# Cross attention of a decoder layer by two matrices made once, in place of query, score, gather and output products

## The chip, the cores and the metric

The kernel runs on one core of one Trainium2 chip. The metric is the device time of one execution in microseconds; lower is better. The core's engines are named as in the profile: PE (matrix products) with PEld (its weight loads), DVE (vector engine), ACT (scalar engine), POOL, and SP, which here only issues transfers. A queue name such as SPq or ACTq stands for the instructions by which an engine issues transfers.

## The reference

One layer of a decoder is computed for a prompt of 1024 tokens and for 8 samples of one token each, all in fp32. The layer has three stages with a residual add behind each: a mixer (attention with forget gates beside a gated unit, then an output projection), cross attention into 256 memory tokens with 4 heads of width 256, and a gated feed-forward network (FFN). The change concerns the cross attention of the prompt:

```
mn = rmsnorm(mem, g_mem)
mk = (mn @ w_ck).reshape(B, M, 4, 256)          # also an output
mv = (mn @ w_cv).reshape(B, M, 4, 256)          # also an output
q  = (xn @ w_cq).reshape(B, T, 4, 256)
s  = einsum('bqhd,bmhd->bhqm', q, mk) / 16
p  = softmax(s)
o  = einsum('bhqm,bmhd->bqhd', p, mv).reshape(B, T, 1024)
x  = x + o @ w_co
```

The products can be taken in another order: q·mkᵀ is xn @ (w_cq · mkᵀ), head by head, and o @ w_co is p @ (mv · w_co), head by head. Both inner matrices have 1024 rows and 1024 columns (256 memory tokens for each of 4 heads) and do not depend on the tokens of the prompt.

## The kernel before

The 1024 prompt tokens are worked in two halves of 512, a half being 4 tiles of 128 tokens. The parts follow in this order: p1 (input projections of the whole prompt), the first half's attention with a filler beside it, the second half's attention, then for each half the output projection of the mixer, the cross attention, and the FFN.

**Products.** Most products are done three times in fp32r, with each operand split into a high part and a low part (`gemm3`, lines 272 to 274: high·high, high·low, low·high). `wload` (lines 252 to 262) brings 256 rows by 512 columns of a weight (512 KB, issued by SP at line 249) into a tile `wr` and splits it: ACT makes the high part `wh` (line 235), DVE the low part `wl` (line 236). `split` with a scale uses lines 238 and 239. Products of the cross attention that take no split are plain fp32.

**The memory projection** `pmem` (line 674) makes mk and mv, 512 columns at a time: 4 weight tiles, then 2 products of 8 k-tiles each, evacuated by ACT (line 711) and stored to the outputs `o_mk` and `o_mv` from ACT's queue (line 712). It is the first part of the filler; `gating(0)` (line 618) is the second. The function `mix` runs the filler beside the first half's attention: for each unit of time that the attention's steps announce, `MIXR` units of the filler are traced, with MIXR 1.0. A part announces its units with `yield`; they are planned figures, not microseconds.

**The cross attention** `cross` (line 1120) of one half does, in order: load mk and mv of two heads (`fetch`, lines 1126 and 1128); load w_cq; normalize and transpose the tokens in two parts of 2 tiles each (`norm_T`, line 1090, transposes at line 1106, splits at 238 and 239), where the first of 8 query blocks is multiplied in two halves of 256 columns as soon as each part is there; the other 7 query blocks with 512 tokens moving and the weight stationary, evacuated by ACT at line 1216; for each head transposes of the keys (`keys`, lines 1153 and 1157), scores in plain fp32 (line 1170) with the softmax (`weigh`: DVE maximum at 1172, exponential on ACT, scaling at 1183), transposes of the softmax weights (`turned`, lines 1190 and 1191), and the gather of values in plain fp32 (`gather`, line 1198), whose result is split for the output projection. `out_proj` (line 1015) multiplies by w_co (lines 1055 to 1057 for the first 512 columns, 1073 to 1075 for the rest), adds the residual, sums squares and makes scaled tiles for the FFN's `norm_T`.

**Beside all of it** runs the work of the 8 samples, first `decode` (attention over 8192 cached tokens: a K step loads 1 MB at line 1407 and is two kinds of DVE operation, lines 1423 and 1427 or 1414 and 1415; a V step loads 1 MB at line 1469 and is 8 products of plain fp32 at line 1475, done in groups of two steps), then `sample_rest` (projections of the 8 rows, with weights loaded by POOL). A driver at the end of `build` takes one step of this work whenever the prompt's parts have announced a given number of units:

```
PACE = {'p1': 7.0, 'att0': 12.0, 'attx': 26.0, 'mid0': 8.0, 'ffn0': 8.5, 'att1': 11.0, 'mid1': 6.8, 'ffn1': 2.5, 'rest': 2.9}
```

`att0` is the first half's attention, `attx` its last two head pairs, `mid0` and `mid1` the output projection and the cross attention of a half, `rest` the samples' remaining work. `beside` and `mix` join other parts.

**Order and buffers.** The code traces the work in the order that these generators give; a planner then simulates it with its own costs and sets the order on each engine, taking work that is ready before work that is not. Buffers are rings of fixed length: 18 tiles `u` of 4 KB a partition, 7 tiles `t2` of 2 KB, 4 `wr`, 5 `wh`, 4 `wl`; result banks of PE are `ba` (4 in this part), `bb` (2), `ms` and `dv`. An instruction that needs a tile waits until the ring's oldest is released.

## Time and profile before

| | |
|---|---|
| median of 3 runs | 1817.83 us (1816.76 to 1819.05) |
| profiled execution | 1820.56 us |
| its span, first to last instruction | 1818.4 us |
| mean granted clock of PE in it | 0.986 |
| moved by DMA | 521.06 MB |

The profile is of one execution. Its page gives the busy time of each engine, the groups of instructions by line, and the chain that ended last; views of the trace give the same for a stretch of time, the instructions in order of time (a row is: start, duration, engine, line, operation, out<-in, count, and in brackets the idle time before it with what ended it), who waited for whom (total, times, longest), and the transfers. In the names out<-in, a matrix product's first operand is the moving one, the second the stationary one. The 8 query evacuations of the second half's cross attention end at about 1262, the first output product after it starts at 1295; in the first half the cross attention lies between 547 and 652.

### The profile page before, as it was taken

What the parts mean: (1) busy time and instruction counts of PE and PEld (TensorE: products, weight loads), DVE (VectorE), ACT (ScalarE), POOL (GpSimd) and SP (SyncE); (2) the same over time, 40 slices, a digit from 0 to 9 for tenths busy, and PEclk for the clock granted to TensorE, in tenths of its full rate; (3) what the DMA queues carried; (4) which work ended last, traced back from release to release, by engine and by line L of the source; (5) the groups of instructions that cost most, each with busy time, mean ns of one, the idle gap of its engine ahead of it and who ended that gap; (6) DMA issues with size and microseconds to landing.
All of it is one profiled execution on the core that took longest, in us unless ns stands there. A gap on an engine that the chain in (4) does not pass through costs nothing.

```text
span 1818.4 us, 25090 instructions
## 1 busy us (share of the span) xinstructions
PE 1745.0 (96%) x9637; PEld 1294.9 (71%) x9637; DVE 1397.5 (77%) x1729; ACT 734.4 (40%) x1378; POOL 510.0 (28%) x461
## 2 busy tenths in 40 slices
PE   8999999888998999999999999989899999999997
PEld 5887776656676767777777776766576778767775
DVE  4689668888788877999989899898875549845344
ACT  6332365455643544433333244235353324332332
POOL 1252334332133432223332333334222111011110
PEclk9999999899999999999999999989999999999999
DMA  8886889777696986679878779988787777568982
GB/s 295 306 297 231 302 297 329 242 266 224 219 398 257 342 310 260 257 285 340 316 279 311 271 306 340 381 300 324 290 309 290 267 268 265 179 266 289 359 314 82
DMA packets 157074, 521.06 MB, mean 287 GB/s; under 512 B 20874, under 2 KB 40842, under 8 KB 124186
## 3 DMA queue, kind: packets, MB, share of 16 engines
q0 software_dynamic: 57168, 341.14, 49.5%
q1 hardware_dynamic: 92874, 165.73, 26.4%
q10 hardware_dynamic: 6912, 12.59, 1.8%
q8 instruction: 76, 1.25, 0.3%
q14 instruction: 44, 0.36, 0.1%
HBM read 495.47 MB, written 23.93 MB: 286 GB/s over the span
## 4 chain that ended last, share of the span: by engine, by line
PE 72%; DMA 10%; issue 7%; DVE 6%; ACT 2%; POOL 2%; SPq 0%; POOLq 0%; DVEq 0%; ACTq 0%
PE ba L272 11%; PE ba L274 11%; PE ba L273 11%; PE bb L272 5%; PE bb L273 5%; PE bb L274 5%; PE dv L1475 5%; DMA kv<-cache_k,io 3%; DMA wr<-w_in 2%; DMA kv<-cache_v,io 1%; PE dv L321 1%; PE dv L1751 1%; PE ba L1056 1%; PE ba L1055 1%; PE ba L1057 1%
## 5 line engine op out<-in xcount | busy, mean ns | idle before, releaser
L235 ACT ACTIVATE wh<-wr 128x1024 fp32r<-128x1024 f32 (+2 forms) x220 | 228.9, 1044 | 489.2 <-PE ba L273 156.0
L236 DVE TENSOR_TENSOR wl<-wr,wh 128x1024 fp32r<-128x1024 f32 (+2 forms) x220 | 262.5, 1200 | 175.6 <-PE ba L274 65.7
L1407 POOL DMA_INDIRECT kv<-cache_k,io x128 | 205.6, 1606 | 551.2 <-DVE s L1427 318.9
L1423 DVE TENSOR_TENSOR kv<-kv,d 128x1024 f32<-128x1024 f32 (+1 forms) x156 | 258.0, 1681 | 35.1 <-DMA kv<-cache_k,io 35.1
L1427 DVE TENSOR_REDUCE s<-kv 128x16 f32<-128x1024 f32 (+1 forms) x156 | 258.2, 1674 | 0.1
L1469 POOL DMA_INDIRECT kv<-cache_v,io x128 | 165.3, 1291 | 282.8 <-PE dv L1475 191.8
L272 PE MATMUL ba<-u,wh 128*128 128x512 f32 (+1 forms) x560 | 220.3, 395 | 1.7 <-ACT u L238 1.7
L273 PE MATMUL ba<-u,wh 128*128 128x512 f32 (+1 forms) x560 | 220.2, 393 | 1.7 <-DVE u L239 1.5
L274 PE MATMUL ba<-u,wl 128*128 128x512 f32 (+1 forms) x560 | 219.5, 393 | 0.0
L272 PE MATMUL ba<-wh,u 128*128 128x512 f32 (+1 forms) x495 | 186.9, 379 | 0.9 <-ACT u L235 0.9
L273 PE MATMUL ba<-wl,u 128*128 128x512 f32 (+1 forms) x495 | 185.4, 375 | 1.2 <-DVE wl L236 1.2
L274 PE MATMUL ba<-wh,u 128*128 128x512 f32 (+1 forms) x495 | 183.8, 376 | 0.0
L272 PEld LDWEIGHTS ba<-u,wh 128*128 128x128 f32 x560 | 106.8, 191 | 30.6 <-issue 5.6
L273 PE MATMUL bb<-u,wh 128*128 128x512 f32 (+1 forms) x304 | 119.4, 393 | 9.2 <-DVE u L239 9.2
L274 PEld LDWEIGHTS ba<-u,wl 128*128 128x128 f32 x560 | 106.9, 191 | 29.1 <-issue 6.1
L273 PEld LDWEIGHTS ba<-u,wh 128*128 128x128 f32 x560 | 106.7, 191 | 27.5 <-issue 2.7
L1475 PE MATMUL dv<-kv,s 128*32 128x512 f32 x1024 | 124.2, 598 | 1.8 <-DMA kv<-cache_v,io 1.8
L272 PE MATMUL bb<-u,wh 128*128 128x512 f32 (+1 forms) x304 | 119.4, 393 | 0.0
L274 PE MATMUL bb<-u,wl 128*128 128x512 f32 (+1 forms) x304 | 118.6, 390 | 0.0
L272 PEld LDWEIGHTS ba<-wh,u 128*128 128x128 f32 x495 | 93.0, 188 | 26.0 <-issue 6.9
L274 PEld LDWEIGHTS ba<-wh,u 128*128 128x128 f32 x495 | 92.8, 188 | 21.5 <-issue 3.7
L273 PEld LDWEIGHTS ba<-wl,u 128*128 128x128 f32 x495 | 93.1, 188 | 19.7 <-DVE wl L236 1.9
(425 smaller groups left out, 3255.9 us busy)
## 6 DMA issues: line engine op xcount, KB each, us to landing
wr<-w_up SPq DMA_DIRECT2D x88, 512.0 KB
kv<-w_up POOLq DMA_DIRECT2D x22, 1024.0 KB, 8.0
wr<-w_down SPq DMA_DIRECT2D x40, 512.0 KB
kv<-w_down POOLq DMA_DIRECT2D x11, 1024.0 KB, 8.5
wr<-w_in SPq DMA_DIRECT2D x16, 512.0 KB
wr<-w_o SPq DMA_DIRECT2D x16, 512.0 KB
wr<-w_cq SPq DMA_DIRECT2D x16, 512.0 KB
wr<-w_co SPq DMA_DIRECT2D x16, 512.0 KB
```

Source lines behind the costliest of these rows:

```text
L235: nc.scalar.activation(h, src, AF.Copy)
L236: nc.vector.tensor_tensor(l, src, h.bitcast(F32), op=ALU.subtract)
L272: mmul(out, sh, mh, start=(i == 0), stop=False)
L273: mmul(out, sh, ml, start=False, stop=False)
L274: mmul(out, sl, mh, start=False, stop=(i == n - 1))
L321: mmul(ps[32 * j : 32 * j + 32, :w], xT[:, k, :] if nk == 8 else xT[:, k * 8 : k * 8 + 32], raw[:, q, j * w : (j + 1) * w], start=(k == 0) ...
L1055: mmul(pss[i], mh[k][:, tb], wh, start=(k == korder[0]), stop=False)
L1407: nc.gpsimd.indirect_dma_start(kv, None, a["cache_k"], off(kidx[:, b, ch : ch + 1]))
L1423: nc.vector.tensor_tensor(kvv[:, i : i + m, :], kvv[:, i : i + m, :], qb.unsqueeze(1).broadcast_to((P, m, 512)), op=ALU.mult)
L1427: nc.vector.tensor_reduce(s[:, ch * 4 + i : ch * 4 + i + m, :].rearrange("p k h -> p (k h)"), kvv[:, i : i + m, :].rearrange("p k (h d) -> ...
L1469: nc.gpsimd.indirect_dma_start(kv, None, a["cache_v"], off(kidx[:, b, ch : ch + 1]))
L1475: mmul(dv[32 * j : 32 * j + 32, :], s[:, ch * 4 : ch * 4 + 4, :].rearrange("p k h -> p (k h)"), kvv[:, j, :], start=(ch == 1), stop=(ch == ...
```

## The change

Two matrices are made once, beside the first half's attention, and kept in device memory: `wk_d` (1024 by 1024: for each head, the head's columns of w_cq times the head's keys transposed) and `wv_d` (1024 by 1024: for each head, the head's values times the head's rows of w_co). The cross attention of each half then multiplies the normalized tokens by `wk_d`, which gives the scores of all heads at once, takes the softmax, transposes the weights and multiplies them by `wv_d` in `out_proj`. The kernel gets the transpose of w_cq as one more input, laid out on the host as others are.

In `pmem` each projected block of 512 columns is read back from the output it was stored to (`fetched`, on SP's queue), transposed on PE and split (`turned`), and multiplied: `into_queries` with 256 columns moving, `into_output` with 512. Results are evacuated by ACT and stored from ACT's queue.

```
-MIXR = 1.0
+MIXR = 1.5
...
+        def project(w, dst, n):
...
+        def fetched(src, n):
+            t = U([P, 2, 512])
+            nc.sync.dma_start(t, src[:, n * 512 : (n + 1) * 512].rearrange("(a p) c -> p a c", p=P))
+            return t
+
+        def turned(t):
+            h2, l2 = U([P, 2, 512], F32R), U([P, 2, 512], F32R)
+            for j in range(2):
+                tr = TR()
+                for dd in range(2):
+                    for mt in range(2):
+                        nc.tensor.transpose(
...
+                split(tr, h2[:, j, :], l2[:, j, :])
+                yield 0.5
+            return h2, l2
+
+        def into_queries(n, h2, l2):
+            for j in range(2):
+                for c in range(2):
+                    w = wload(wpair(a["w_cqT"], n * 2 + j, c * 512, 512), 1024)
+                    for q in range(2):
+                        ps = MM()
+                        for i in range(2):
+                            mb = slice((q * 2 + i) * P, (q * 2 + i + 1) * P)
+                            gemm3(
+                                ps[:, i * 256 : (i + 1) * 256],
+                                [
+                                    (w[0][:, d_, mb], w[1][:, d_, mb], h2[:, j, d_ * 256 : d_ * 256 + 256], l2[:, j, d_ * 256 : d_ * 256 + 256])
+                                    for d_ in range(2)
+                                ],
+                            )
+                        t = T2()
+                        nc.scalar.activation(t, ps, AF.Copy)
+                        r0, c0 = c * 512 + q * 256, (n * 2 + j) * 256
+                        nc.scalar.dma_start(
+                            wk_d[r0 : r0 + 256, c0 : c0 + 256].rearrange("(a p) k -> p a k", p=P), t.rearrange("p (a k) -> p a k", k=256)
+                        )
+                    yield 2.9
+
+        def into_output(n, h2, l2):
+            for j in range(2):
+                for c in range(2):
+                    w = wload(wpair(a["w_co"], n * 2 + j, c * 512, 512), 1024)
+                    for mt in range(2):
+                        ps = MM()
...
+                        t = T2()
+                        nc.scalar.activation(t, ps, AF.Copy)
+                        r0 = (n * 2 + j) * 256 + mt * P
+                        nc.scalar.dma_start(wv_d[r0 : r0 + P, c * 512 : (c + 1) * 512], t)
+                    yield 2.9
+
+        for w, dst, into in ((a["w_ck"], mk_d, into_queries), (a["w_cv"], mv_d, into_output)):
+            raws = []
             for n in range(2):
+                yield from project(w, dst, n)
+                raws.append(fetched(dst, n))
+            for n in range(2):
+                h2, l2 = yield from turned(raws[n])
+                yield from into(n, h2, l2)
```

`project` holds what the loop of `pmem` did before. In `norm_T`, what is done behind each of the two parts may now be a generator. In `cross`, tokens are stationary and the matrix moves, 512 columns (two heads) for each of the 4 token tiles; the softmax of a tile follows its product, and the transposes of an earlier tile's weights stand between the products:

```
     def cross(xt, sq):
+        loaded = lambda n: [wload(wpair(wk_d, kk, n * 512, 512), 1024) for kk in range(4)]
+        ws = loaded(0)
...
+        def scores(i, hs, ls):
+            ps, tb = MM(), slice(i * P, (i + 1) * P)
             gemm3(
+                ps,
+                [(hs[k][:, tb], ls[k][:, tb], ws[k // 2][0][:, k % 2, :], ws[k // 2][1][:, k % 2, :]) for k in range(8)],
             )
+            return ps
+
+        def weigh(n, i, ps):
...
+            pp = T2().rearrange("p (j m) -> p j m", m=256)
...
+        def turned():
...
+            split(tr, oh[n, i // 2][:, :, c], ol[n, i // 2][:, :, c])
+
+        def first(hs, ls, c):
+            i0 = c.start // P
+            r = rows_rstd(sq, i0, i0 + 2)
+            nc.vector.tensor_scalar(rq[:, i0 : i0 + 2], r, 1.0 / 16, None, op0=ALU.mult)
+            for i in (i0, i0 + 1):
+                weigh(0, i, scores(i, hs, ls))
                 yield 5.2
+
+        hs, ls = yield from norm_T(xt, G_CROSS, first)
+        ws = loaded(1)
+        for i in range(4):
+            ps = scores(i, hs, ls)
+            turned()
+            weigh(1, i, ps)
+            yield 5.6
+        turned()
...
+        yield from out_proj(wv_d, of, xt, ys=ys, between={0: turned, 1: turned, 2: turned})
```

The functions `fetch`, `products`, `keys` and `gather` go, and with them the query block in memory, the plain fp32 scores and the plain fp32 gather. `out_proj` takes its stationary tiles through a function `of(k, i)` and can call a function behind a given k (`between`). The samples' own cross attention is not changed, and `o_mk` and `o_mv` are written as before.

More of the change, by code (lines that the diff above doesn't have):

```diff
@@ L1112, in norm_T @@
                 yield 0.6
-            first(hs, ls, c)
-            if t0 == 0:
+            more = first(hs, ls, c)
+            if more:
+                yield from more
+            elif t0 == 0:
                 yield 3
@@ L1134, in cross @@
-        q2, ps0 = [], MM()
-        def products(out, ws, dt_, hs, ls, c):
-            cb = slice(dt_ * P, (dt_ + 1) * P)
+        loaded = lambda n: [wload(wpair(wk_d, kk, n * 512, 512), 1024) for kk in range(4)]
+        ws = loaded(0)
+        rq = sm([P, 4], "rq", 2)
+        oh, ol, weights = {}, {}, []
+        def scores(i, hs, ls):
+            ps, tb = MM(), slice(i * P, (i + 1) * P)
             gemm3(
-                out,
-                [(ws[k // 2][0][:, k % 2, cb], ws[k // 2][1][:, k % 2, cb], hs[k][:, c], ls[k][:, c]) for k in range(8)],
-            )
@@ L1224, in cross @@
-        keys(2)
-        fetch(3)
-        turned(0)
-        yield 1
-        weigh(2)
-        yield 3
-        gather(0)
-        yield 4
-        keys(3)
-        turned(1)
-        yield 1
-        weigh(3)
-        yield 3
-        gather(1)
-        yield 4
-        for h in (2, 3):
-            turned(h)
-            yield 1
-            gather(h)
-            yield 4
+                ps,
+                [(hs[k][:, tb], ls[k][:, tb], ws[k // 2][0][:, k % 2, :], ws[k // 2][1][:, k % 2, :]) for k in range(8)],
+            )
@@ new lines, in turned @@
+        def turned():
+            n, i, pp = weights.pop(0)
+            if i % 2 == 0:
+                oh[n, i // 2], ol[n, i // 2] = U([P, 4, 256], F32R), U([P, 4, 256], F32R)
+            c = slice(i % 2 * P, i % 2 * P + P)
+            tr = TR().rearrange("p (k t) -> p k t", t=P)
+            for k in range(4):
+                nc.tensor.transpose(tr[:, k, :], pp[:, k // 2, k % 2 * P : k % 2 * P + P], ident)
+            split(tr, oh[n, i // 2][:, :, c], ol[n, i // 2][:, :, c])
[5 more added lines that the diff above has]
+                weigh(0, i, scores(i, hs, ls))
+                yield 5.2
```

169 lines of the change are left out of this document (55 added, 114 removed).

## The prediction

> **What bounds the kernel now.** I read the page's busy line first, then the windows by stage, the order of time on TensorE (PE), and the waits.
>
> ```profile
> PE 1745.0 (96%) x9637; PEld 1294.9 (71%) x9637; DVE 1397.5 (77%) x1729; ACT 734.4 (40%) x1378; POOL 510.0 (28%) x461
> ```
> ```profile
> 262.00:365.00 103.00, 92.37 (x522) 69.03 (x525) 84.03 (x155) 57.07 (x134) 41.69 (x55) 0.95 0.78 272
> 488.00:547.00 59.00, 58.38 (x309) 44.39 (x308) 48.84 (x60) 26.09 (x45) 17.78 (x12) 1.00 1.00 383
> 547.00:652.00 105.00, 98.36 (x508) 70.35 (x506) 89.00 (x116) 53.18 (x125) 38.52 (x25) 0.97 0.84 316
> 1183.00:1296.00 113.00, 99.67 (x502) 69.78 (x502) 96.00 (x114) 52.72 (x122) 41.71 (x29) 0.94 0.83 306
> 708.00:1110.00 402.00, 398.57 (x1884) 298.60 (x1883) 372.10 (x357) 147.07 (x237) 117.48 (x83) 0.99 0.79 298
> ```
>
> The columns are length, busy PE, weight load, VectorE (DVE), ScalarE (ACT), POOL, then clock, DMA share and GB/s. The rows are the first attention with the memory projection beside it (262 to 365), the first half's output projection, its cross attention, the second half's cross attention, and the first FFN. PE is occupied nearly everywhere, so the sum of PE work sets the time. DVE is next: 0.93 of the FFN row (372.1/402), 0.85 of both cross rows.
>
> A matmul's duration contains its latency. What one costs in a stream is the distance between starts.
>
> ```profile
> 571.86 0.39 PE L272 MATMUL bb<-u,wh 128*128 128x512 f32 x1
> ...
> 576.28 0.40 PE L274 MATMUL ba<-u,wl 128*128 128x512 f32 x1
> ```
> ```profile
> 76.33 0.28 PE L273 MATMUL bb<-wl,u 128*128 128x260 f32 x1
> ...
> 78.00 0.28 PE L272 MATMUL bb<-wh,u 128*128 128x260 f32 x1
> ```
> ```profile
> 633.03 0.63 PE L1153 MATMUL ba<-cp,t 128*128 128x128 f32 x4 [0.34 <-DMA t<-o_mk]
> 633.49 0.60 PE L1190 MATMUL ba<-cp,u 128*128 128x128 f32 x4
> ...
> 635.45 3.72 PE L1170 MATMUL ba<-t,u 128*128 128x256 f32 x16 [0.68 <-ACT t L1157]
> 639.01 1.02 PE L1198 MATMUL bb<-u,t 128*128 128x512 f32 x2
> 639.87 1.02 PE L1198 MATMUL ba<-u,t 128*128 128x512 f32 x2
> ```
>
> In fp32r, 20 starts from 571.86 to 576.28 give 0.233 us for 512 columns. 15 starts from 76.33 to 78.00 give 0.119 for 260 columns, though each shows 0.28. The transposes take 0.115 (0.46/4). Plain fp32 takes two records for one matmul: line 1170 0.2225 each (3.56/16), line 1198 0.43 each (0.86/2).
>
> **What goes, what comes, on PE.** Query products (192 a half), transposes of the weights (32 a half) and output products (192 a half) keep their columns. Gone are the fp32 scores, 64 matmuls, 128 records × 0.2225 = 28.5 us; the fp32 gather, 32 matmuls, 64 × 0.43 = 27.5; and the key transposes, 32 × 0.115 = 3.7. That is 59.7, half of it in each cross stage. New, once, beside the first attention: 192 products of 256 columns × 0.119 = 22.8; 96 of 512 × 0.233 = 22.4; 32 transposes = 3.7. That is 48.9. Net **−11 us**. Were a 256-column product worth its shown duration, 0.28, it would be 54 instead of 22.8 and the net +20; the starts decide, so I take 0.119.
>
> **Waits that go.**
>
> ```profile
> PE bb L1170 <- DVE u L236: 4.2, 1, 4.2
> PE ba L1170 <- ACT t L1157: 1.9, 2, 1.6
> PE bb L1198 <- ACT u L1191: 0.6, 1, 0.6
> PE ba L1198 <- ACT u L1191: 0.6, 1, 0.6
> ```
> ```profile
> 1278.40 3.64 PE L1170 MATMUL bb<-t,u 128*128 128x256 f32 x8 [4.19 <-DVE u L236]
> ```
> ```profile
> PE bb L273 <- DVE u L239: 9.2, 5, 5.6
> ```
>
> The first four rows are all PE waits of the second half's cross products. They lie in the chains keys-scores and transpose-gather, which cease: −7.3. Behind the 4.19 us gap eight records took 3.47 us up to the next start (1281.87), twice the normal, so the gap cost 1.7 more. **−9** in all; the first half's are shorter and not counted. In the new order a weight tile is turned four tiles after its softmax, with 24 products (5.6 us) a tile between, so a turn should wait for nothing. The last row, of the whole execution, is the split of the normalized tiles. Its waits were covered by 24 half products (2.8 us); now two whole score tiles (11 us) stand between the two halves of that part. I take half: **−5**, bounds 0 and −9.
>
> **What the first attention takes on.**
>
> ```profile
> L235 ACT ACTIVATE wh<-wr 128x1024 fp32r<-128x1024 f32 (+2 forms) x220 | 228.9, 1044 | 489.2 <-PE ba L273 156.0
> L236 DVE TENSOR_TENSOR wl<-wr,wh 128x1024 fp32r<-128x1024 f32 (+2 forms) x220 | 262.5, 1200 | 175.6 <-PE ba L274 65.7
> ```
> ```profile
> L711 ACT ACTIVATE t<-ba,rm x5: 687/687/691, 268.5 to 323.6; 128x512 f32<-128x512 f32 x5
> ```
> ```profile
> L712 ACTq DMA_DIRECT2D o_mk<-t x4: 338/342/345, 269.2 to 293.6; - x4
> ```
> ```profile
> DMA packets 14123, 28.05 MB, mean 272 GB/s; under 512 B 1368, under 2 KB 7000, under 8 KB 12579
> ...
> ks_d<-u POOLq DMA_DIRECT2D x12, 128.0 KB, 3.6
> ```
>
> 16 weight loads are split (ACT 16.7 us, DVE 19.2), 32 results evacuated (ACT 22) and stored from ACT's queue (32 × 0.34 = 11), and 8 key and value blocks split (5 each). ACT rises by 55 to 112 us of some 150, DVE from 84 by 24, and by the decode steps below. All of it hides beside PE as long as these engines keep up; uncovered, a part would cost its own length. The higher ratio lets the filler, 41.6 planned units before and about 92 now, last through the whole attention. The gaps of 103 − 92.4 = 10.6 us come partly from the filler running out. I take **−4**, bounds 0 and −10.6. The reads of the two projected blocks wait on SP for the stores. They could hold back the weight loads behind them for one store's landing, some 4 us by the last row above (of half the size), four times. The planner issues what is ready by its own costs, not in the code's order:
>
> ```profile
> 485.39 7.64 SPq L249 DMA_DIRECT2D wr<-w_o  x5
> 493.08 1.12 SPq L1126 DMA_DIRECT2D t<-o_mk  x1
> ...
> 503.36 4.74 SPq L249 DMA_DIRECT2D wr<-w_o  x2
> ```
>
> The load of the memory keys went out amid the w_o loads, which the code asks for first. So I take 0, bound +16. New loads and stores by ACT in the cross stages: none.
>
> **Decode, which is paced by planned units.** The added filler is about 50 units: at 12 and 26 units a step, some 3 steps (bounds 2 and 4) are done earlier. Each cross stage yields about 27 units less: 3.4 steps fewer at 8 in the first, 4 at 6.8 in the second. This only moves work, until the end:
>
> ```profile
> L1475 PE MATMUL dv<-kv,s x144: 592/592/617, 1369.4 to 1432.0; 128*32 128x512 f32 x144
> ```
> ```profile
> 1792.98 0.73 DVE L1804 SCALAR_TENSOR_TENSOR vsum<-vsum,r1r,d 8x512 f32<-8x512 f32 x1
> ```
> ```profile
> 1806.33 1.19 DVE u L1340
> ```
>
> Four steps more remain behind 1363, about 10 units at 2.5. The sample's last result stands 13 us ahead of the prompt's, so I count 0, bound +5.
>
> **DVE in the cross stages.**
>
> ```profile
> L1427 DVE TENSOR_REDUCE s<-kv 128x16 f32<-128x1024 f32 x22 | 26.3, 1212 | 0.0
> L1423 DVE TENSOR_TENSOR kv<-kv,d 128x1024 f32<-128x1024 f32 x22 | 25.9, 1216 | 5.5 <-DMA kv<-cache_k,io 5.5
> ```
>
> Here a key step of decode is two of each, 4.86 us. DVE falls by 3.4 × 4.86 = 16.5 to 72.5, and in the second half by 19.4 to 76.6, while PE falls to about 69. DVE is then the fuller engine. At the FFN's share of 0.926 the two stages need 78 + 83 = 161 instead of 218, a gain of 57, where PE alone would allow 59.7 + 14 = 74. The neighbours at 0.83 can take some. I charge half the difference, **+9**, bounds 0 and +17.
>
> **Sum**: −11 − 9 − 5 − 4 + 9 = −20. The profiled execution took 1820.56 us (span 1818.4), the median of the runs is 1817.83, 0.15% lower: 1800.6, at the median's level **1798**. A difference of 0.2%, 3.6 us, is about what a measurement of this kernel can tell from no change.
>
> **Rivals.**
> *Result buffers run short, slower.* In the first attention the evacuated results use the ring of 7 t2 tiles, with the exponentials and transposes of the attention. Each result holds one for 0.69 + 0.34 + at least 3.6 = 4.6 us; 32 need 147 buffer-us. Their stretch lasts about 62 us (45 of products, 17 of attention: the 47.7 us left of 92.4 after 192 × 0.233, for 70 units, times 31 units). So 2.4 buffers must be free. The attention can hold six (three exponentials, two transposed, one output). With 1.5 free the stretch takes 98 us: +36, net +16, **1834**. It turns slower below 147/(62 + 20) = 1.8 free. For it: ACT is to be the busiest server there. Against: the planner gives buffers by readiness, and before, line 711 waited only for PE.
> The Trainium skill, "DMA: Bandwidth & Descriptors", section "Anatomy of one DMA", puts a DMA at 2.0 us plus its bytes over 436 GB/s, with the receipt from HBM as most of it. That would be an estimated 2.6 us for a store of 256 KB and a threshold nearer 1.4; the trace's 3.6 us for 128 KB is longer.
> *Transfers bind the first attention.* 16 loads and the same bytes stored are 16.8 MB, the blocks read back 2.1, three steps of K and V 6.3: 28 becomes 53.2 MB. At 383 GB/s that is 139 us, less than PE's 103 + 48.9 + 3 − 4 = 151. At 316, the rate of the cross row, it is 168: +17, **1815**, no change. The stage ran at 272, though only because it asked for no more.
> The Trainium skill, same page, section "Bandwidth", gives some 358 GB/s of HBM per core as the limit. By it the stage needs an estimated 149 us, as much as PE. The 383 GB/s row disagrees.
> *DVE binds the cross stages outright*: the whole +17, **1806**.
> *The waits go entirely*: −11 − 9 − 9 − 10.6, **1778**.
>
> **Chances.** Forecast 0.40 (own range 1787 to 1806), DVE 0.15, all waits gone 0.07: faster 0.62. Transfers 0.10: same. Buffers 0.28: slower. The range runs from the best case to the slower one: 1779 to 1834.
>
> **What would show it.** Right: lines of the scores and gather vanish; the cross stages shrink to about 80 us; the first attention grows to about 150 with PE above 0.93; PE's busy sum falls by about 11. Wrong: the first attention beyond 180 us with ACT waiting for t2 tiles or stores; DVE above 0.95 in the cross stages with PE waiting for splits; sample work behind the prompt's last output.

## The result: slower by 25 us

The changed kernel took 1843.49 us (median of 4 runs, 1840.09 to 1846.3), the kernel before in the same comparison 1818.44 (1816.76 to 1822.79): ratio **1.0137**, 95% interval [1.0111, 1.0164]. The forecast was 1798 with a range up to 1834; the time lies outside the range, and the change is slower where faster was forecast. The profiled execution of the changed kernel took 1840.93 us, span 1839.2.

The busy line of its page answers to the one of before:

```profile
PE 1741.9 (95%) x9685; PEld 1297.8 (71%) x9685; DVE 1423.2 (77%) x1769; ACT 754.8 (41%) x1382; POOL 502.8 (27%) x463
```

PE is 3.1 us less busy and the span 20.8 us longer, so PE's idle time grew by 23.9 us. PE's granted clock fell too, from 0.986 to 0.977 in the mean. As an estimate by these means, PE had 1702 us of full-speed work (1741.9 × 0.977) where before had 1721 (1745.0 × 0.986), 19 us less, and at the old clock it would have been busy some 16 us less than it was. No run separates whether the lower clock costs time of its own or only follows the idle time.

The windows say where the time went. A stage begins at the first product of an output projection or at the first transpose of a normalization. First come three stages of before (both attentions; first FFN, here FFN 0; second FFN to the end, here FFN 1), then the same of after, with an output projection and both cross stages; columns as in the prediction.

```profile
262.00:497.10 235.10, 208.27 (x1332) 148.44 (x1332) 193.32 (x341) 138.59 (x310) 78.28 (x102) 0.96 0.74 250
...
706.60:1135.30 428.70, 422.86 (x2019) 315.63 (x2017) 395.33 (x383) 162.36 (x264) 128.34 (x89) 0.99 0.80 300
...
1350.80:1818.40 467.60, 455.75 (x2979) 339.98 (x2977) 266.89 (x403) 157.57 (x287) 71.74 (x101) 0.99 0.70 256
```
```profile
262.00:577.00 315.00, 269.29 (x1692) 197.43 (x1691) 235.77 (x388) 182.31 (x372) 87.99 (x109) 0.93 0.80 275
577.00:627.90 50.90, 50.89 (x227) 38.57 (x228) 45.15 (x57) 13.11 (x23) 20.42 (x12) 0.96 0.86 324
627.90:687.00 59.10, 57.50 (x296) 43.89 (x294) 45.78 (x74) 35.66 (x86) 9.68 (x9) 1.00 0.61 227
...
744.10:1180.90 436.80, 428.05 (x2053) 317.58 (x2053) 408.15 (x398) 164.15 (x265) 139.13 (x96) 0.99 0.83 305
...
1227.70:1290.60 62.90, 60.61 (x313) 44.30 (x311) 52.99 (x77) 34.24 (x81) 22.42 (x17) 0.97 0.69 256
...
1350.60:1839.20 488.60, 468.96 (x3045) 343.25 (x3045) 301.82 (x432) 163.61 (x292) 92.51 (x118) 0.98 0.76 280
```

The cross stages fell from 104.2 and 112.9 us (at these cuts) to 59.1 and 62.9, which is 95 us and more than was forecast. The attentions grew by 79.9, the first FFN by 8.1, the second by 21.0, the output projections and what follows them by 6.9 together. The sum is +20.8. FFN 1 begins at the same time in both (1350.8 and 1350.6): up to there the other stages take back all that the cross stages win, and what is lost on top is lost in FFN 1.

The table counts the decode's key steps in each stage (a step is one key load; one that lies across a cut counts on both sides), and gives the lengths of the same stages in four kernels of the experiments: without the samples' work, and with half of a key step's VectorE work left out. "op" is an output projection: a and c are the mixer's of the two halves, b and d the cross attention's.

| stage | before, us (key steps) | after, us (key steps) | before, no samples | after, no samples | before, half key | after, half key |
|---|---|---|---|---|---|---|
| attentions | 235.1 (15) | 315.0 (18) | 197.8 | 257.6 | 248.4 | 322.2 |
| op a | 50.5 | 50.9 | 46.1 | 45.3 | 47.8 | 49.3 |
| cross 0 | 104.2 (11) | 59.1 (3) | 92.5 | 52.5 | 100.9 | 59.0 |
| op b | 54.8 | 57.1 | 48.4 | 47.5 | 54.8 | 54.0 |
| FFN 0 | 428.7 (42) | 436.8 (46) | 377.9 | 376.5 | 422.1 | 427.3 |
| op c | 47.3 | 46.8 | 44.6 | 44.6 | 48.9 | 48.8 |
| cross 1 | 112.9 (13) | 62.9 (7) | 86.5 | 50.7 | 98.5 | 60.0 |
| op d | 55.3 | 60.0 | 46.6 | 45.8 | 55.1 | 52.0 |
| FFN 1 to the end | 467.6 (0) | 488.6 (6) | 381.9 | 382.0 | 467.2 | 485.5 |

Two readings of the changed kernel's trace belong beside it. All waits of PE in its first cross stage, and then in its second:

```profile
PE bb L274 <- DVE u L1078: 0.9, 1, 0.9
PE ba L274 <- issue: 0.4, 1, 0.4
PE ba L276 <- DVE u L241: 0.3, 1, 0.3
```
```profile
PE bb L276 <- DVE u L241: 2.3, 1, 2.3
```

The chains keys-scores and transpose-gather are gone with their waits. And VectorE's key steps in those stages: in the second cross stage of before, then in the first and the second of after:

```profile
L1423 DVE TENSOR_TENSOR kv<-kv,d 128x1024 f32<-128x1024 f32 x28 | 33.0, 1219 | 8.6 <-DMA kv<-cache_k,io 8.6
L1427 DVE TENSOR_REDUCE s<-kv 128x16 f32<-128x1024 f32 x27 | 31.8, 1208 | 0.0
```
```profile
L1436 DVE TENSOR_TENSOR kv<-kv,d 128x1024 f32<-128x1024 f32 x6 | 7.0, 1212 | 0.0
L1440 DVE TENSOR_REDUCE s<-kv 128x16 f32<-128x1024 f32 x5 | 5.9, 1208 | 0.0
```
```profile
L1440 DVE TENSOR_REDUCE s<-kv 128x16 f32<-128x1024 f32 x12 | 14.3, 1209 | 0.0
L1436 DVE TENSOR_TENSOR kv<-kv,d 128x1024 f32<-128x1024 f32 x12 | 14.1, 1214 | 0.0
```

The first cross stage of before had 22 of each. Of its 52 us of key work (the prediction's rows) 13 are left there, of the second's 65 us 28. That work, 76 us, had to be done elsewhere: by the loads 24 key steps lay in the two stages, now 10.

### The profile page after: what moved, and what is told of

Same layout as the page of the kernel before. It is cut to its first block, busy times and chain, and to the rows that moved or that the text cites. A ratio compares the mean times of both kernels' runs of the same rounds, so it can differ in the third digit from the quotient of the medians.

```text
span 1839.2 us, 25344 instructions
## 1 busy us (share of the span) xinstructions
PE 1741.9 (95%) x9685; PEld 1297.8 (71%) x9685; DVE 1423.2 (77%) x1769; ACT 754.8 (41%) x1382; POOL 502.8 (27%) x463
## 4 chain that ended last, share of the span: by engine, by line
PE 58%; DVE 9%; DMA 4%; issue 4%; ACT 1%; POOL 1%; DVEq 0%; POOLq 0%; ACTq 0%; SPq 0%
PE ba L274 9%; PE ba L275 8%; PE ba L276 8%; PE dv L1488 5%; PE bb L274 4%; PE bb L276 4%; PE bb L275 4%; DVE kv L1436 1%; DMA kv<-cache_k,io 1%; DVE s L1440 1%; DMA d<-cache_logf,lidx 1%; PE dv L323 1%; PE dv L1764 1%; DVE wl L238 1%; PE ba L1126 1%
## 5 line engine op out<-in xcount | busy, mean ns | idle before, releaser
L237 ACT ACTIVATE wh<-wr 128x1024 fp32r<-128x1024 f32 (+2 forms) x236 | 245.6, 1045 | 493.2 <-PE ba L275 159.2
L238 DVE TENSOR_TENSOR wl<-wr,wh 128x1024 fp32r<-128x1024 f32 (+2 forms) x236 | 282.5, 1201 | 148.7 <-PE ba L276 61.2
L1420 POOL DMA_INDIRECT kv<-cache_k,io x128 | 191.5, 1496 | 576.1 <-DVE s L1440 312.7
L1436 DVE TENSOR_TENSOR kv<-kv,d 128x1024 f32<-128x1024 f32 (+1 forms) x149 | 253.1, 1724 | 19.3 <-DMA kv<-cache_k,io 19.2
L274 PE MATMUL ba<-wh,u 128*128 128x512 f32 (+1 forms) x582 | 222.7, 385 | 8.0 <-DVE u L1332 6.8
L275 PE MATMUL ba<-wl,u 128*128 128x512 f32 (+1 forms) x582 | 221.3, 382 | 1.3 <-DVE wl L238 1.3
L276 PE MATMUL ba<-wh,u 128*128 128x512 f32 (+1 forms) x582 | 219.3, 381 | 1.0 <-DVE u L238 0.7
L275 PE MATMUL ba<-u,wh 128*128 128x512 f32 (+1 forms) x552 | 212.1, 385 | 3.0 <-DVE u L241 3.0
L274 PE MATMUL ba<-u,wh 128*128 128x512 f32 (+1 forms) x552 | 211.3, 386 | 1.2 <-ACT u L240 1.2
L274 PEld LDWEIGHTS ba<-wh,u 128*128 128x128 f32 x582 | 110.3, 190 | 38.8 <-DVE u L1332 7.3
L276 PEld LDWEIGHTS ba<-wh,u 128*128 128x128 f32 x582 | 110.3, 190 | 28.0 <-issue 5.2
L275 PEld LDWEIGHTS ba<-wl,u 128*128 128x128 f32 x582 | 110.3, 190 | 27.8 <-issue 4.2
L274 PE MATMUL bb<-wh,u 128*128 128x512 f32 (+1 forms) x314 | 121.4, 387 | 2.9 <-DVE u L1078 2.8
L276 PE MATMUL bb<-wh,u 128*128 128x512 f32 (+1 forms) x314 | 120.1, 383 | 2.3 <-DVE u L241 2.3
L276 PEld LDWEIGHTS ba<-u,wl 128*128 128x128 f32 x552 | 104.2, 189 | 24.1 <-issue 4.4
L275 PE MATMUL bb<-wl,u 128*128 128x512 f32 (+1 forms) x314 | 120.1, 383 | 0.0
```

The costliest lines, as they stand in the source:

```text
L237: nc.scalar.activation(h, src, AF.Copy)
L238: nc.vector.tensor_tensor(l, src, h.bitcast(F32), op=ALU.subtract)
L274: mmul(out, sh, mh, start=(i == 0), stop=False)
L275: mmul(out, sh, ml, start=False, stop=False)
L276: mmul(out, sl, mh, start=False, stop=(i == n - 1))
L1420: nc.gpsimd.indirect_dma_start(kv, None, a["cache_k"], off(kidx[:, b, ch : ch + 1]))
```

## The experiments

**The decode theory**: the decode steps that leave the cross stages are the loss. There they lay beside prompt work that left VectorE room; now they lie where it has less. **Rivals**: the making itself costs far more than its products (result buffers, read-back); the pace constants are merely wrong for the new lengths; what the late value steps need (PE time, transfers) is the loss and not VectorE.

The texts on record use letters, and not the same ones throughout. In those of e1 to e8, A is the making and B the decode theory. In those of e12 and e13, B1 is the lost VectorE room, B2 the PE time and the transfers of late steps. In those of e15 to e18, A is the VectorE room, B1 the late value products, B2 the late transfers.

### One half of the change alone, and the read-back

`e1_make_only` is the kernel before with the changed kernel's `pmem`, `MIXR = 1.5`, and the old cross stages; the matrices are made and not used. `e2_use_only` has the new cross stages without the making, on plain weights:

```
-        loaded = lambda n: [wload(wpair(wk_d, kk, n * 512, 512), 1024) for kk in range(4)]
+        loaded = lambda n: [wload(wpair(a["w_cq"], kk, n * 512, 512), 1024) for kk in range(4)]
...
-        yield from out_proj(wv_d, of, xt, ys=ys, between={0: turned, 1: turned, 2: turned})
+        yield from out_proj(a["w_co"], of, xt, ys=ys, between={0: turned, 1: turned, 2: turned})
```

`e3_no_readback` keeps each projected block in SBUF (`project` evacuates into a U tile, and `fetched` goes).

> The kernel before with the two matrices made and stored beside the first attention (ratio 1.5), but not used: the cross attention is the old one, so the new matrices are extra work. Theory A (the making is what costs: the stage of the first attention cannot take the work at its PE price of 49 us): 65 to 85 us over the kernel before, 1883 to 1903 us. Theory B (the making costs its PE work and no more, and the loss comes from decode steps that the shorter cross stages no longer carry): 40 to 55 us over, 1858 to 1873 us.

> The changed kernel without the making: the cross attention multiplies by w_cq and w_co in the places of the two matrices, so its result is not the layer's; the filler and its ratio are those of before. Theory A: the cross stages shrink by 45 and 50 us and nothing is given back, 80 to 95 us under the kernel before, 1723 to 1738 us. Theory B: decode steps leave the cross stages and cost PE and transfer time behind them, 25 to 45 us of the 95 are lost in the FFN stages, 1748 to 1768 us.

> The changed kernel, but the projected keys and values stay in an on-chip u tile that is stored to the output and turned from there; no block is read back. If the wait of SP for the stores and the extra 2 MB hold up the filler (a part of theory A): 5 to 15 us under the changed kernel, 1828 to 1838 us. If not: within 4 us of 1843.

Measured: e1 1882.0 us, ratio 1.0356 [1.0333, 1.0378], +65 over the 1817.02 of before; e2 1786.69, 0.9824 [0.9801, 0.9848], −30; e3 1843.0, 1.0139 [1.0114, 1.0164]. The making costs 65 us where its products were put at 48.9, the use gains only 30 of the 102 us by which its two stages shrink (56.0 and 58.7 us in e2). e1 lies at the lower end of what its text gave for the making; e2 lost more than either of its two theories allowed. The read-back costs nothing: without it the time is the same.

The attentions of e1, then the first and the second FFN of e2:

```profile
262.00:578.70 316.70, 272.73 (x1695) 200.58 (x1693) 236.14 (x388) 183.98 (x376) 83.74 (x109) 0.92 0.80 275
```
```profile
668.70:1112.60 443.90, 427.88 (x2039) 317.64 (x2036) 411.32 (x398) 159.47 (x261) 141.56 (x97) 0.98 0.81 302
1272.70:1786.30 513.60, 477.81 (x3078) 345.73 (x3077) 315.10 (x442) 162.88 (x290) 105.30 (x126) 0.96 0.77 282
```

With the old cross stages e1 has the attentions of the changed kernel (316.7 and 315.0 us, 18 key steps in both), so their length comes with the making and not with steps that left the cross stages. In e2 FFN 0 is 15.2 us longer than before and FFN 1 46.0, which has 10 key loads and 28 value loads where before had 0 and 14. The end of e2 is no longer set by the prompt: from 1657 to 1773 the chain that ended last goes through the loads of the samples' projection weights.

```profile
1657.34 8.32 DMA kv<-w_up
...
1765.37 7.85 DMA kv<-w_down
```

The samples' last store is issued at 1780.3 there, the prompt's last at 1781.7: late decode steps make the samples' remaining work late, too.

### Pace constants

`e4_pace_mid` sets the pace of the changed kernel's cross stages from 8.0 and 6.8 units a step to 5.0 and 4.6, meant to give them about as many steps as before. `e8_pace_att` sets 9, 11 and 8 for the first attention, between them, and the second (12, 26, 11). `e14_pace_even` sets 16 for attx, 7.0 and 6.4 for the cross stages, 9 for the second attention. `e5_before_pace` does the opposite to the kernel before: cross stages at 9.0 and 7.6.

```
-PACE = {..., 'att0': 12.0, 'attx': 26.0, 'mid0': 8.0, ..., 'att1': 11.0, 'mid1': 6.8, ...}
+PACE = {..., 'att0': 9.0, 'attx': 11.0, 'mid0': 8.0, ..., 'att1': 8.0, 'mid1': 6.8, ...}
```

> The changed kernel with a decode step per 5.0 units in place of 8.0 in the first half's output projection and cross attention and per 4.6 in place of 6.8 in the second's, which puts back about as many steps as the cross stages lost. Theory B: the last FFN gets its old length back (about 20 us less) and the cross stages grow by less, 8 to 20 us under the changed kernel, 1823 to 1835 us. Theory A: what the last FFN gains the cross stages lose, within 4 us of 1843, or slower by DVE in the cross stages.

> The kernel before, with a decode step per 9.0 units in place of 8.0 in the first half's output projection and cross attention and per 7.6 in place of 6.8 in the second's: some five decode steps leave these stages for the last FFN, as many as in the changed kernel, and nothing else is touched. Theory B (a decode step that comes late costs more than it frees): the last FFN grows by 15 to 25 us and the stages ahead shrink by less, 5 to 15 us over the kernel before, 1822 to 1832 us. Theory A: within 4 us of 1817.

> The changed kernel with more decode beside both attentions: a step per 9 units in place of 12, per 11 in place of 26 in the first attention's second half, and per 8 in place of 11 in the second attention; some ten steps come earlier. Those stages have 46 us of PE idle and DVE at 0.75. Theory B: no K steps are left for the last FFN, which falls back to 468 us or under, and the attention stages grow by less, 1815 to 1832 us. Theory A: the attention stages, already held by their buffers and chains, grow by as much as is gained, within 5 us of 1843 or over.

> The changed kernel with the decode spread anew: a step per 16 units in place of 26 in the first attention's second half, 9 in place of 11 in the second attention, 7 in place of 8 and 6.4 in place of 6.8 around the cross stages. If the price of a step is much the same wherever it now lies (2 to 3 us), no pacing wins back the loss: 1828 to 1838 us. If the place matters: under 1825.

Measured: e4 1837.24, 1.01 [1.0078, 1.0123]; e8 1833.09, 1.0079 [1.0059, 1.0099]; e14 1846.69, 1.0168 [1.0144, 1.0193]; e5 1831.33, 1.0075 [1.0056, 1.0095]. e4 came out between its two ranges, e8 within 2 us of the decode theory's, e14 in neither. In e4 FFN 1 is back at 468.2 us with no key step left in it, but the new cross stages took no more than 7 and 7, and FFN 0 took 454.1 with 49.

The kernel before loses 14 us when only its pace is loosened, as the decode theory had it (5 to 15). Its cross stages kept 10 and 13 key loads. Two key steps left the first half's output projections, and the last FFN took 478.5 us with 20 value loads in place of 467.6 with 14. In e8 the attentions and the second FFN read:

```profile
262.00:598.60 336.60, 281.05 (x1766) 200.50 (x1764) 280.73 (x466) 182.87 (x375) 111.36 (x126) 0.92 0.87 307
1367.40:1832.40 465.00, 454.03 (x2978) 339.19 (x2978) 265.21 (x405) 158.96 (x288) 71.12 (x101) 0.99 0.70 258
```

The second FFN is as short as before (465.0), since no key step is left for it; but the 8 key steps more in the attentions cost 21.6 us there, 2.7 a step (with the value steps that go with them). In the old cross stages 24 steps cost 38.1 us by the table (11.7 and 26.4, with less without the samples), 1.6 a step. So another pace wins some 10 of the 25 us (e8), and none that was tried wins more.

### No samples' work at all

`e6_before_nodec` and `e7_after_nodec` leave all work of the samples out of both kernels, the decode and the projections behind it (`bgs.append(sample())` goes).

> The kernel before without any work of the samples (their attention over the cache and their projections are left out, and their outputs are not written). It serves as the base of the next kernel. PE loses 128 V steps of 0.93 us and the samples' projections; some 1500 to 1620 us by both theories.

> The changed kernel without any work of the samples, to be set against the kernel before without it. Theory B (the loss is the decode's): faster than that base by the net of the products and the waits of the cross stages, 10 to 25 us. Theory A (the first attention cannot take the making at its price): the making's 65 to 80 us stand against 60 us of products and the waits, so from 5 us under to 20 us over that base.

Measured on one chip: e6 1585.99 us, 0.8719 [0.8701, 0.8737] of before; e7 1566.29, 0.8612 [0.8595, 0.8628]. **Without the samples' work the change gains 19.7 us**, as the decode theory had it (10 to 25). The attentions and the two cross stages of e6, then of e7:

```profile
262.00:459.80 197.80, 181.16 (x1157) 135.37 (x1155) 111.45 (x199) 129.11 (x288) 38.55 (x68) 0.97 0.44 133
505.90:598.40 92.50, 85.47 (x406) 66.56 (x404) 34.78 (x61) 50.72 (x123) 1.00 (x1) 0.98 0.29 97
1069.30:1155.80 86.50, 80.75 (x389) 63.14 (x388) 28.84 (x48) 50.69 (x120) 1.01 (x1) 1.00 0.22 73
```
```profile
262.00:519.60 257.60, 233.72 (x1488) 182.19 (x1487) 139.45 (x228) 170.95 (x356) 38.81 (x68) 0.96 0.57 180
564.90:617.40 52.50, 52.13 (x262) 43.20 (x260) 30.36 (x58) 34.01 (x84) 0.70 (x1) 1.00 0.31 101
1086.00:1136.70 50.70, 50.33 (x245) 41.31 (x243) 25.98 (x47) 34.10 (x81) 0.70 (x1) 1.00 0.23 74
```

The cross stages lose 40.0 and 35.8 us, the making adds 59.8. VectorE's own room, the length less its busy time, was 57.7 + 57.7 = 115 us in the old cross stages and is 22.1 + 24.7 = 47 in the new: 68 us of room are gone. The key work that left is of like size, 14 steps of 4.86 us by the loads; that the room set their number is not shown, and e13 below speaks against it. By stage (the table, with the samples' work less without), this work costs 234.1 us before and 274.7 after. It rises by 20.1 us in the attentions, 9.5 in FFN 0 and 20.9 in FFN 1, and falls by 5.1 and 14.2 in the cross stages; the output projections add 9.4.

Beside e1 and e2 this says which half of the change loses. The making costs 65 us with the samples' work and 59.8 without. The use gains 30 with it and 79.5 without (19.7 + 59.8). So the samples' work takes 5 us from the first half and 49 from the second; together the two lose less than this sum, 45.

### Half of a key step's VectorE work

`e12_before_halfk` and `e13_after_halfk` leave out the multiplication by the query in each key step, and with it half of the step's 4.86 us on VectorE; loads, values and softmax stay.

```
-                    nc.vector.tensor_tensor(
-                        kvv[:, i : i + m, :], kvv[:, i : i + m, :], qb.unsqueeze(1).broadcast_to((P, m, 512)), op=ALU.mult
-                    )
```

> The kernel before with half of the DVE work of a decode K step: the product of the keys with the query is left out and only the sum is taken (the samples' attention is then not the layer's). Loads, V steps and everything else stay. DVE loses some 2.4 us for each of 128 steps. Where DVE is not the bound this changes little: 20 to 80 us under the kernel before. It is the base of the next kernel.

> The changed kernel with the same half left out of the K steps. Theory B1 (the old cross stages had DVE time to spare in which K steps lay; the new ones have not, and the steps pushed out cost): with half the DVE price the new stages hold their steps again, and the changed kernel comes out 10 to 20 us under its base, as without any decode. Theory B2 (what costs is the PE time and the transfers of the steps that come late): both are as before, so it stays 15 to 30 us over its base.

Measured on one chip: e12 1808.9, 0.9961 [0.9948, 0.9974]; e13 1816.3, 0.9993 [0.9982, 1.0003]. The same cut is worth 8 us to the kernel before (20 to 80 were expected) and 27 to the changed one, and the difference between them falls from +25 to +7.4. (The table's two lengths differ by 14.4, since e13's profiled execution, 1821.86 us, is the slowest of its ten.) Neither theory's text came true: the changed kernel is not under its base, and not 15 us over it. The cross stages of e13:

```profile
633.50:692.50 59.00, 56.49 (x294) 43.73 (x292) 38.60 (x67) 35.56 (x86) 8.30 (x9) 1.00 0.64 235
1222.60:1282.60 60.00, 58.92 (x295) 42.62 (x294) 41.90 (x67) 35.51 (x83) 14.37 (x15) 1.00 0.75 282
```

They hold 3 and 7 key loads, as in the changed kernel (11 and 12 in e12), though VectorE is busy only two thirds of the time. So the room on VectorE does not decide how many steps lie there; what the steps cost on VectorE has a share in the loss. Between the −19.7 without the samples' work and the +25 with it lie 45 us, and half of the key steps' VectorE work takes 18 of them away. If the loss were all VectorE's key work and in proportion to it, half would be 22; with intervals of about 2 us a run the two are close, but the proportion is assumed and not shown. The next pair asks for the value steps' share.

### The value steps

`e15_before_thinv` and `e16_after_thinv` cut the four products of a value step to one of 128 columns (the loads stay; the result bank is set to zero first). `e17_before_novload` and `e18_after_novload` drop the value loads and keep the products, on a constant tile.

```
-                    for j in range(4):
-                        mmul(dv[32 * j : 32 * j + 32, :], ..., kvv[:, j, :], ...)
+                    j = ch % 4
+                    mmul(dv[32 * j : 32 * j + 32, :128], ..., kvv[:, j, :128], ...)
```

> The kernel before, with every V step's four products of 512 columns cut to one product of 128 columns (its V loads stay): most of the decode's V products are left out. 1680 to 1790 us: 672 V steps' products of some 0.9 us each lie in the whole trace, partly idle time of the tensor engine. It is the base of e16. Theory A (what is lost is room on the vector engine for K steps): the change costs the same +20 to +30 us with the products gone. Theory B1 (the late V steps' products cost tensor time behind a prompt that is short of it): the difference after minus before falls to +10 us or under. Theory B2 (transfers): it stays at +15 to +30.

> The changed kernel with the same cut of the V products. Theory A: 20 to 30 us above e15. Theory B1: 10 us above e15 or less. Theory B2: 15 to 30 us above e15.

> The kernel before without its V loads: the V products stay, on a constant tile in place of the loaded rows; half of the decode's transfers are left out. 1700 to 1815 us, the base of e18. Theory B2 (the late V loads crowd the weight loads of the feed-forward of layer 1): the difference after minus before falls to +10 us or under. Theories A and B1: it stays at +15 to +30 us.

> The changed kernel without its V loads, V products on a constant tile. Theory B2: 10 us above e17 or less. Theories A and B1: 15 to 30 us above e17.

(The number of value steps in the first of these texts is wrong: it is 128, with 1024 records and 124.2 us in the group of line 1475.) Measured on one chip: e15 1801.85, 0.9931 [0.9904, 0.9957]; e16 1835.86, 1.0111 [1.0074, 1.0148]; e17 1863.72, 1.0266 [1.0237, 1.0296]; e18 1835.91, 1.0118 [1.009, 1.0147].

(e15 and e17 lie above what was expected of them, 1680 to 1790 and 1700 to 1815.) With thin products the change costs 34 us, and not 10 or less as the theory of the late value products had it (VectorE's had 20 to 30). Up to FFN 1 the pair differs as the full kernels do: it begins at 1327.6 in e15 and at 1328.9 in e16, so the thin products give nothing back there. For FFN 1 itself, 31.6 us longer in e16, the pair does not tell. From 1706 on e16's chain that ended last goes through the samples' projection weights, as in e2, while e15's goes through PE's products:

```profile
1706.20 9.33 DMA kv<-w_up
...
1808.48 9.50 DMA kv<-w_down
```

In the changed kernel FFN 1 has 64 value records more than before (the rows are in the next section). At 0.121 us each (124.2/1024) that is 7.8 of the 13.2 us by which PE is busier there (468.96 and 455.75). So up to some 8 of the 25 us may be the late products'. The first FFN of e15 shows VectorE's part:

```profile
706.50:1138.70 432.20, 401.65 (x1766) 316.58 (x1765) 397.40 (x387) 160.74 (x261) 137.25 (x89) 0.96 0.80 297
```

Against the row of before, PE has 21 us less to do (401.65 and 422.86), VectorE as much (397.40 and 395.33), and the stage is no shorter (432.2 and 428.7, at a granted clock of 0.96 and 0.99). It is VectorE that holds its length: PE's waits for it there sum to 18.0 us, where before had 3.9. The largest of them:

```profile
PE bb L272 <- DVE u L1319: 8.7, 2, 5.1
```

In e12, where VectorE has 318 us there, the stage takes 422.1, all but 1.6 of it PE. In the full kernels both engines are near their limit in this stage, and PE is the fuller (408.15 us of VectorE and 428.05 of PE in the changed kernel's 436.8).

The pair without value loads tells nothing on transfers. Its base moved: the kernel before became 49 us slower by losing half of its decode's transfers. POOL's waits for a key buffer, in before and then in e17, show that something else changed:

```profile
POOL kv L1407 <- DVE s L1427: 318.9, 69, 27.0
```
```profile
POOL kv L1407 <- DVE s L1427: 729.2, 93, 29.9
```

Key and value loads share four buffers. With no value loads between them, key loads wait for VectorE more than twice as long, and the cross stages take 121.6 and 122.7 us; how the one leads to the other is not shown. The difference after less before turned to −28 us, but more than the transfers changed. Whether late transfers have a share of the loss stays open.

### The making: buffers, its place, its density

`e9_u_evac` evacuates the results of both makings into U tiles in place of the t2 ring; `e10_mix2` sets `MIXR` to 2.0; `e11_split_att` makes the values' matrix beside the second attention (`MIXR` 1.2, 0.4 there).

```
+                    tt = U([P, 2, 512])
...
-                        t = T2()
+                        t = tt[:, q, :]
```

> The changed kernel, but the 32 results of the two new matrices are evacuated into u tiles (two to a tile) in place of the t2 ring; nothing else differs. If the ring of 7 t2 tiles is what makes the first attention's stage longer than its PE work (the recorded rival of result buffers): 10 to 20 us under the changed kernel, 1823 to 1833 us, with the 12 us wait of PE behind a store gone. If the stage is long for other reasons: within 4 us of 1843.

> The changed kernel with the ratio 2.0 in place of 1.5: the filler ends sooner, so that the gating, which ran behind the first attention, runs beside it, and the attention's own tail is left with less filler. If the stage's idle time comes from the filler running past the attention: 5 to 12 us under the changed kernel, 1831 to 1838 us. If it is spread over both attentions: within 4 us of 1843.

> The changed kernel with the second matrix (values times output weight) made beside the second attention at the ratio 0.4, the rest beside the first at 1.2. The second attention's stretch has idle PE that the filler could use. If a stage takes work cheaply where PE idles: both attentions together shrink by 10 to 20 us, 1823 to 1833 us. If buffers or decode steps set the length: within 4 us of 1843 or slower.

Measured: e9 1853.93, 1.0193 [1.0169, 1.0216]; e10 1848.73, 1.0167 [1.0145, 1.019]; e11 1876.46, 1.032 [1.0288, 1.0351]. None is better, and e9 is slower than both of its texts allowed. In e10 the attentions do shrink, from 315.0 to 308.8, but the two FFNs take 445.8 and 496.8. There is one place in the changed kernel where the t2 ring did bite, at the end of the making:

```profile
PE bb L934 <- ACT t L923: 12.3, 2, 6.6
...
ACT t L923 <- DMA wv_d<-t: 6.4, 1, 6.4
```

The attention's output tile waited 6.4 us for a store of the values' matrix to free a tile, and PE for it. In e9 that wait for the store is gone, but PE waits 6.8 us for the same tile and ACT 5.5 us for a load of `ks_d`, and the attentions take 322.8. So the rival of the short buffers names a wait that exists, of some 6 to 12 us; e9 does not show it to be the loss, though its own buffers may cost what the ring did. No version that makes the matrices and does the samples' work beats the kernel before.

## Why the prediction was wrong

**What held.** The PE terms: the 256-column products of the making start 0.116 us apart (0.93 us over the 8 starts between these rows of the changed kernel), as taken (0.119), though each shows 0.28:

```profile
309.75 0.28 PE L274 MATMUL ba<-u,wh 128*128 128x256 f32 x1
...
310.68 0.28 PE L276 MATMUL ba<-u,wl 128*128 128x256 f32 x1
```

The cross stages' terms were −59.7, −9 and −5, −73.7 in all; without the samples' work the two stages lost 75.8, of which 63.8 are PE's busy time and 12.0 its idle time. PE's busy time over the whole kernel fell by 14.2 there (1535.6 to 1521.4), where 11 was forecast. The first attention with the making, forecast at about 150 us, took 158, though PE was less full than the 0.93 foretold (142.56/158 = 0.90):

```profile
262.00:420.00 158.00, 142.56 (x835) 109.34 (x836) 114.79 (x179) 91.56 (x179) 51.50 (x63) 0.96 0.88 311
```

The read-back was rightly put at 0: SP waited for the stores of `o_mk` 5.4 us in all, and e3 shows that it did not matter.

**What was mis-sized: the making's uncovered parts.** They were counted at 0 beside 48.9 us of products, with −4 for the gaps that the filler was to close. Without the samples' work the attentions grew by 59.8: PE's busy time by 52.6 (233.72 − 181.16) and its idle time by 7.2, where −4 was forecast. So the term is +59.8 in place of +44.9, 15 us off. The sum without its decode term was −11 − 9 − 5 − 4 = −29; on the chip it was −19.7: 15 lost here, 2 won in the cross stages and 4 in the other stages of the table.

**What failed: the samples' work, the decode above all.** The step reads "This only moves work, until the end", with 0 and a bound of +5, and the term "DVE in the cross stages" charged +9, bound +17, for VectorE's fuller share. Together they allow +22; measured were 45 us (from −19.7 to +25.05). Three things were wrong in it.

- *The count.* Pace units gave 7.4 steps fewer in the cross stages. The trace has 24 and 10: 14 fewer. Why is open; e13 has the same number with VectorE a third idle.
- *The price.* The step lets a step of decode cost the same wherever it lies. By the table the 14 steps freed 19.3 us in the cross stages, 1.4 a step. The FFNs and the output projections took some 12 more, and the samples' work in them grew by 39.8, 3.3 a step. An average hides this: FFN 0 had 42 steps for 50.8 us before, 1.2 each, and four more cost 9.5. The attentions add 20.1, beside the making and with it. That is −19.3 + 39.8 + 20.1 = 40.6 (274.7 − 234.1). These prices hold all of the samples' work in a stage; e12 and e13 put some 18 of the 45 us on the key steps' VectorE work.
- *The place looked at.* VectorE was watched in the cross stages, where it was to reach the FFN's share of 0.93. It fell to 45.78/59.1 = 0.77 and 52.99/62.9 = 0.84: the steps did not squeeze in there, they left. The loss came in the attentions, in FFN 0 and in the stage that no later one can absorb, FFN 1.

The end of the decode shows it. Value products and the sample's last store in the changed kernel:

```profile
L1488 PE MATMUL dv<-kv,s x208: 592/592/1058, 1359.1 to 1491.7; 128*32 128x512 f32 x104
```
```profile
L1818 SPq DMA_DIRECT2D o_ys<-vsum x1: 298/298/298, 1826.8 to 1826.8; - x1
```

208 value records stand behind 1350 where 144 stood behind 1363 before, and the last of them comes at 1491.7, not 1432.0. The sample's output is still some 12 us ahead of the end (25 before: 1793.7 of 1818.4), so the named sign "sample work behind the prompt's last output" did not come in the changed kernel; e2, with no making to hold the prompt up, is at its edge. The loss showed as prompt stages made longer, which the prediction did not look for.

The rivals: transfers (1815) put the first attention at 168 us, where it took 158. "DVE binds the cross stages" (1806) named a resource that matters, but in the wrong stage. The buffers' rival (1834) had the sign and came nearest to the time, by another mechanism, which e9 does not support: that is luck. The figure behind its 2.6 us a store is given in the Trainium skill, "DMA: Bandwidth & Descriptors", section "Anatomy of one DMA", for transfers issued by POOL; ACT issues these stores, and the traces here do not show when they land.

**What stays open**: how the other 27 of the 45 us divide among the late value products (up to 8), the value loads (e17 and e18 do not separate them), the samples' late projections and the lower clock; why 14 steps left and not 7; and why the making idles PE 7 us more without the samples' work.

## What to carry to other kernels

Background work that hides beside a stage has no fixed price, and the average of a stage does not tell what one more step costs there. Before a stage is shortened, ask which hidden work it carries, where that goes, and how full the engines are in that place. Here 76 us of prompt work went from the cross stages, 14 key steps went elsewhere, and a gain of 20 became a loss of 25. Run both kernels without the background work once: it splits the forecast into the part that is understood and the part that isn't.

## What was not expected of the hardware

PE's granted clock fell when PE was given less to do. The cores view of before, then of e15:

```profile
core 0: 1818.4 us, clock 0.986
```
```profile
core 0: 1800.1 us, clock 0.963
```

Its page has PE busy 1680.2 us where before had 1745.0. At the granted clocks that is 1618 us of full-speed work in place of 1721: 103 us of work went, 65 of busy time and 13 of the median (18 of the span). The attentions show it best: the clock of 262 to 500 was 0.90 in e15 and 0.96 before. The Trainium skill, "TensorE: Matmul & The Clock Gate", section "Part 1: The HAM clock gate", has the clock follow how busy PE has lately been; these rows agree: with the value products gone, PE had less to do and the clock fell.
